# One transfer of a mask's diagonal blocks cut into four and spread between the large loads of a matmul-softmax kernel

## Chip, cores, metric

One core of a Trainium2 chip. The metric is device time of one execution in microseconds (us). A span of the profile is some 1.8 us shorter than the device time of the same execution.

## The reference

```python
batch, m, k, n = 16, 512, 512, 512
y = scale * np.matmul(x, weight)          # x [16, 512, 512], weight [512, 512], float32
y = np.where(mask == 1, y, -1e9)          # mask [512, 512], ones strictly below the diagonal
y_exp = np.exp(y - np.max(y, axis=-1, keepdims=True))
return y_exp / np.sum(y_exp, axis=-1, keepdims=True)
```

Input x is 16 MB, the output 16 MB, the weight 1 MB. Of the mask only the four diagonal blocks of 128 x 128 are read, 256 KB: the rest of it is known to both kernels.

## The kernel before

A unit is 1 MB of x: a half (256 rows) of two batches. There are 16 units, x0 to x15. For each, the SP queue loads 128 partitions x 8 KB, VectorE casts to bf16, TensorE transposes in 16 steps, VectorE and ScalarE evict half each, TensorE multiplies with the weight and adds the mask as one more product (`band`), ScalarE takes the exponential with its row sum, VectorE normalises, and the SP queue stores 1 MB.

The mask's path, with cuts:

```python
diag_r = bass.AP(tensor=mask.tensor, offset=mask.offset,
                 ap=[[N, P], [P * N + P, KT], [1, P]])   # 128 partitions, 4 rows of 512 B each
...
load(0)
seq(nc.sync.dma_start(diag_f32, diag_r))
seq(nc.sync.dma_start(w_f32, weight.rearrange("(p kt) n -> p kt n", kt=KT)))
for u in range(1, X_BUFS):                               # X_BUFS = 8
    load(u)
...
cast(0)
seq(nc.vector.tensor_scalar(out=diag_bf, in0=diag_f32, ...))     # 0/1 -> -512/0
transpose(0)
evict(0)
for t in range(T):
    # pm = spread[:, t] x diag_bf, then two copies of 64 rows into band
    ...
# casts of the weight, cast(1)
for u in range(U + 1):
    if u + 1 < U:
        transpose(u + 1)
    if u + 2 < U:
        cast(u + 2)
    if u + 1 < U:
        evict(u + 1)
    if u < U:
        multiply(u)
    if u >= 1:
        normalise(u - 1)
        store(u - 1)
        if u - 1 + X_BUFS < U:
            load(u - 1 + X_BUFS)
```

The softmax here doesn't subtract the row's maximum and nothing guards it: scores larger than these inputs give would overflow.

Of the kernel before, what the change touches and what calls it, by code (L numbers as in the profile page):

```python
# [8 lines left out]
FP32 = mybir.dt.float32  # L9
BF16 = mybir.dt.bfloat16  # L10
AF = mybir.ActivationFunctionType
ALU = mybir.AluOpType

MASK_NEG = -512.0
P = 128
X_BUFS = 8
# [5 lines left out]
def kernel(  # L22
# [15 lines left out]



    nc = tc.nc

    B, M, K = x.shape
    K2, N = weight.shape
    assert K == K2 and N == 512 and K == 512 and M == 512 and B % 2 == 0
    KT = K // P
    T = 4
    HP = P // 2
    HB = 2 * P
    U = B  # L50
# [7 lines left out]
    psum_y = ctx.enter_context(tc.tile_pool(name="psum_y", bufs=4, space=bass.MemoryType.PSUM))  # L58

    x_r = x.rearrange("(c e) (h p t) k -> c h p e (t k)", e=2, h=2, t=T)  # L60
    out_r = out.rearrange("(c e) (h p t) n -> c h p e (t n)", e=2, h=2, t=T)

    diag_r = bass.AP(tensor=mask.tensor, offset=mask.offset, ap=[[N, P], [P * N + P, KT], [1, P]])

    ident_bf = const.tile([P, P], BF16, name="ident_bf")
    w_f32 = const.tile([P, KT, N], FP32, name="w_f32")
    w_bf = const.tile([P, KT, N], BF16, name="w_bf")
    diag_f32 = const.tile([P, KT, P], FP32, name="diag_f32")
    diag_bf = const.tile([P, KT, P], BF16, name="diag_bf")
    spread = const.tile([P, T, P], BF16, name="spread")  # L70
    zeros = const.tile([P, N], BF16, name="zeros")
    band = const.tile([P, 2, T, HB], BF16, name="band")
# [3 lines left out]
    seq = tc.keep_in_program_order  # L76

    def load(u):
        xf = x_pool.tile([P, T, K], FP32, name="xf")
        seq(nc.sync.dma_start(xf.rearrange("p t k -> p (t k)"), x_r[u // 2, u % 2]))  # L80
        st_x[u] = xf

    def cast(u):
        xb = xb_pool.tile([P, T, K], BF16, name="xb")
        seq(nc.vector.tensor_copy(xb, st_x.pop(u)))  # L85
        st_xb[u] = xb

    def transpose(u):
        xb = st_xb.pop(u)
        st_pt[u] = [psum_t.tile([P, 2, T, P], BF16, name="pt") for _ in range(2)]  # L90
        for kt in range(KT):
            for t in range(T):
                seq(
                    nc.tensor.transpose(  # L94
                        st_pt[u][kt // 2][:, kt % 2, t],
                        xb[:, t].rearrange("p (k kt) -> p kt k", kt=KT)[:, kt],
                        ident_bf,
                    )
                )

    def evict(u):
        xt = xt_pool.tile([P, KT, T, P], BF16, name="xt")
        pt = st_pt.pop(u)
        seq(nc.vector.tensor_copy(xt[:, 0:2], pt[0]))  # L104
        seq(nc.scalar.copy(xt[:, 2:4], pt[1]))  # L105
        st_xt[u] = xt

    def multiply(u):
        h = u % 2
        NC = (h + 1) * HB  # L110
        xt = st_xt.pop(u)
        ot = ots[u % OUT_BUFS]
        rsum = sum_pool.tile([P, T], FP32, name="rsum")
        for t in range(T):
            py = psum_y.tile([P, N], FP32, name="py")
            for kt in range(KT):
                seq(
                    nc.tensor.matmul(  # L118
                        py[:, :NC],
                        lhsT=xt[:, kt, t],  # L120
                        rhs=w_bf[:, kt, :NC],
                        start=(kt == 0),
                        stop=(kt == KT - 1),
                    )
                )
            seq(
                nc.tensor.matmul(  # L127
                    py[:, h * HB : NC],
                    lhsT=ident_bf,
                    rhs=band[:, h, t],  # L130
                    start=False,
                    stop=True,
                    skip_group_check=True,
                )
            )
            seq(
                nc.scalar.activation(  # L137
                    out=ot[:, t, :NC],
                    in_=py[:, :NC],
                    func=AF.Exp,  # L140
                    bias=0.0,
                    scale=float(scale),
                    accum_out=rsum[:, t : t + 1],
                )
            )
        st_sum[u] = rsum

    def normalise(u):
        ot = ots[u % OUT_BUFS]
        NC = (u % 2 + 1) * HB  # L150
        rinv = sum_pool.tile([P, T], FP32, name="rinv")
        seq(nc.vector.reciprocal(rinv, st_sum.pop(u)))  # L152
        for t in range(T):
            seq(nc.vector.tensor_scalar_mul(ot[:, t, :NC], ot[:, t, :NC], rinv[:, t : t + 1]))  # L154
        if u % 2 == 0:
            seq(nc.gpsimd.memset(ot[0:2, 0, :HB], 1.0 / N))  # L156

    def store(u):
        ot = ots[u % OUT_BUFS]
        seq(nc.sync.dma_start(out_r[u // 2, u % 2], ot.rearrange("p t n -> p (t n)")))  # L160


    load(0)
    seq(nc.sync.dma_start(diag_f32, diag_r))  # L164
    seq(nc.sync.dma_start(w_f32, weight.rearrange("(p kt) n -> p kt n", kt=KT)))  # L165
    for u in range(1, X_BUFS):
        load(u)


# [13 lines left out]
    for g in range(2):  # L183
        for e in range(2):
# [4 lines left out]
                )  # L189
            )  # L190

    cast(0)
    seq(
        nc.vector.tensor_scalar(  # L194
            out=diag_bf,
            in0=diag_f32,
            scalar1=-MASK_NEG,
            scalar2=MASK_NEG,
            op0=ALU.mult,
            op1=ALU.add,  # L200
        )
    )
    transpose(0)
    evict(0)
    for t in range(T):
        pm = psum_y.tile([P, N], FP32, name="py")
        seq(
            nc.tensor.matmul(  # L208
                pm, lhsT=spread[:, t], rhs=diag_bf.rearrange("k b c -> k (b c)"), start=True, stop=True
            )  # L210
        )
        for g, copy in enumerate((nc.vector.tensor_copy, nc.scalar.copy)):
            half = slice(g * HP, (g + 1) * HP)
            src = pm.rearrange("p (h g c) -> p h g c", h=2, g=2)
            seq(copy(band[half, :, t, g * P : (g + 1) * P], src[half, :, g]))  # L215
    seq(nc.vector.tensor_copy(w_bf[:, 0:2], w_f32[:, 0:2]))
    seq(nc.scalar.copy(w_bf[:, 2:4], w_f32[:, 2:4]))
    cast(1)
# [1 line left out]
    for u in range(U + 1):  # L220
        if u + 1 < U:
            transpose(u + 1)
        if u + 2 < U:
            cast(u + 2)
        if u + 1 < U:
            evict(u + 1)
        if u < U:
            multiply(u)
        if u >= 1:
            normalise(u - 1)  # L230
            store(u - 1)
            if u - 1 + X_BUFS < U:
                load(u - 1 + X_BUFS)
# [35 lines left out]
```

## Time and profile before

| what | value | view |
|---|---|---|
| device time | 90.92 us (90.89 to 90.98) | three executions |
| span | 89.1 us | page |
| DMA moved | 34.95 MB, 392 GB/s over the span | page |
| DMA rate in the body | 416 to 438 GB/s | strip of 40 slices |
| TensorE busy | 72.0 us, 81% | page |
| last arithmetic, last landing | 82.0, 88.1 us | timeline, waits of the DMA queue |

How to read it: the strips cut the span into 40 slices of 2.2 us; a digit is a busy share in tenths. A stretch has its bounds and length first, then the busy time of each engine, and last the granted clock of TensorE, the DMA share and GB/s. In a timeline, a line is start, duration, engine, line of the kernel, operation, `out<-in`, and in brackets how long the engine had been idle and what ended that. The lines themselves stand in the prediction below.

Besides what those views show, the trace holds for every transfer 16 landing records, one for each DMA engine.

### The profile page before, as it was taken

The page shows a single profiled execution, that of the slowest core. Times are in us where ns is not written, and L with a number is a line of the kernel's source. Part 1 is how long each engine was busy: PE and PEld are TensorE (multiplying, and loading weights), DVE is VectorE, ACT ScalarE, POOL GpSimd, SP SyncE. Part 2 cuts the span into 40 slices and gives each one's busy share as a digit, 9 for nine tenths or more (in the row PEclk, how much of TensorE's full clock was granted, in tenths as well). Part 3 has the DMA queues.
Part 4 walks back from the last instruction along what each step waited for, and adds up shares of the span by engine and source line. Part 5 has one row for each costly group of instructions (what it writes and reads, how often), then busy time and mean ns, then how long its engine had stood idle before and what let it go on. Part 6 is the DMA issues. An engine that isn't in the chain of part 4 may idle for free.

```text
span 89.1 us, 1610 instructions
## 1 busy us (share of the span) xinstructions
PE 72.0 (81%) x584; PEld 49.4 (56%) x592; DVE 60.5 (68%) x123; ACT 55.3 (62%) x154; POOL 7.3 (8%) x20
## 2 busy tenths in 40 slices
PE   4996205999999999999999999999999999960000
PEld 1325005767489569758955975795598578520000
DVE  5885914756849959994996899599685948607000
ACT  5403830646779778687977877797687869660000
POOL 7620000000100200020020002001000100200000
PEclk9999995559999999999999999999999999998555
DMA  0859999999999999999999999999999999999970
GB/s 11 324 204 381 419 434 427 423 423 430 416 419 419 423 430 430 419 419 423 423 427 430 430 416 419 430 434 423 416 427 430 419 416 430 438 416 434 423 313 22
DMA packets 5287, 34.95 MB, mean 392 GB/s; under 512 B 545, under 2 KB 1057, under 8 KB 1057
## 3 DMA queue, kind: packets, MB, share of 16 engines
q1 hardware_dynamic: 5280, 34.87, 93.9%
q8 instruction: 4, 0.07, 0.3%
q14 instruction: 3, 0.02, 0.0%
HBM read 18.09 MB, written 16.78 MB: 391 GB/s over the span
## 4 chain that ended last, share of the span: by engine, by line
PE 73%; DMA 12%; DVE 3%; SPq 2%; issue 1%; ACT 1%; DVEq 0%; ACTq 0%
PE py L118 48%; PE pt L94 16%; DMA xf<-in_x_dram 12%; PE py L127 8%; DVE ot L154 1%; DVE xb L85 1%; SPq L80 1%; ACT ot L137 1%; SPq L164 1%; SPq L165 1%; DVEq L264 0%; DVE rinv L152 0%; ACTq L264 0%
## 5 line engine op out<-in xcount | busy, mean ns | idle before, releaser
L118 PE MATMUL py<-w_bf,xt 128*128 128x256 bf16 (+1 forms) x248 | 51.0, 333 | 0.4
L137 ACT ACTIVATE ot<-py 128x256 f32<-128x256 f32 (+1 forms) x64 | 31.2, 493 | 8.9 <-PE py L127 8.8
L118 PEld LDWEIGHTS <-xt 128*128 128x128 bf16 x256 | 25.2, 101 | 12.7
L105 ACT COPY xt<-pt 128x1024 bf16<-128x1024 bf16 x16 | 16.2, 1013 | 14.7 <-PE pt L94 10.1
L154 DVE TENSOR_SCALAR ot<-ot,rinv 128x256 f32<-128x256 f32 (+1 forms) x64 | 23.5, 431 | 0.8
L85 DVE CAST xb<-xf 128x2048 bf16<-128x2048 f32 x16 | 19.5, 1220 | 5.9 <-DMA xf<-in_x_dram 5.9
L94 PE MATMUL pt<-ident_bf,xb 128*128 128x128 bf16 x256 | 17.8, 225 | 5.3 <-DVE xb L85 5.3
L94 PEld LDWEIGHTS <-xb 128*128 128x128 bf16 x256 | 16.6, 115 | 7.7 <-DVE xb L85 6.7
L127 PE MATMUL py<-band,ident_bf 128*128 128x256 bf16 x64 | 18.0, 281 | 0.0
L104 DVE COPY xt<-pt 128x1024 bf16<-128x1024 bf16 x16 | 11.0, 688 | 8.9 <-PE pt L94 8.9
L137 ACT ACTIVATION_READ_ACCUMULATOR ot<-py 128x1 f32 x64 | 12.8, 200 | 0.0
L156 POOL MEMSET ot<- 2x256 f32 x8 | 3.6, 448 | 67.7 <-DVE ot L154 67.7
L127 PEld LDWEIGHTS <-ident_bf 128*128 128x128 bf16 x64 | 6.5, 101 | 4.4
L173 PE MATMUL py<-zeros 128*128 128x512 bf16 x12 | 5.3, 632 | 1.2 <-DVE zeros L170 1.2
L152 DVE RECIPROCAL rinv<-rsum 128x4 f32<-128x4 f32 x16 | 2.7, 169 | 3.2 <-ACT ot L137 3.2
L179 DVE MEMSET ot<- 128x1024 f32 x4 | 3.6, 912 | 0.6 <-issue 0.6
L173 PEld LDWEIGHTS <-zeros 128*128 128x128 bf16 x12 | 1.6, 144 | 3.9 <-issue 2.8
L186 ACT ACT_TABLE_LOAD x1 | 1.3, 1283 | 0.7 <-PEq L250 0.7
L215 ACT CAST band<-py 64x256 bf16<-64x256 f32 x4 | 1.4, 368 | 0.2 <-DVE band L215 0.2
L215 DVE CAST band<-py 64x256 bf16<-64x256 f32 x4 | 1.4, 406 | 0.0
L208 PE MATMUL py<-diag_bf,spread 128*128 128x512 bf16 x4 | 1.0, 377 | 0.4 <-DVE diag_bf L194 0.4
L180 POOL MEMSET ot<- 2x256 f32 x4 | 1.2, 302 | 1.5 <-DVE ot L179 1.4
(14 smaller groups left out, 6.6 us busy)
## 6 DMA issues: line engine op xcount, KB each, us to landing
xf<-in_x_dram SPq DMA_DIRECT2D x16, 1024.0 KB, 13.9
out_dram<-ot SPq DMA_DIRECT2D x16, 1024.0 KB, 10.6
w_f<-in_weight_dram SPq DMA_DIRECT2D x1, 1024.0 KB, 8.4
diag_f<-in_mask_dram SPq DMA_DIRECT2D x1, 256.0 KB, 6.5
```

Of the source, the lines that this page charges most:

```text
L85: seq(nc.vector.tensor_copy(xb, st_x.pop(u)))
L94: nc.tensor.transpose(st_pt[u][kt // 2][:, kt % 2, t], xb[:, t].rearrange("p (k kt) -> p kt k", kt=KT)[:, kt], ident_bf,)
L104: seq(nc.vector.tensor_copy(xt[:, 0:2], pt[0]))
L105: seq(nc.scalar.copy(xt[:, 2:4], pt[1]))
L118: nc.tensor.matmul(py[:, :NC], lhsT=xt[:, kt, t], rhs=w_bf[:, kt, :NC], start=(kt == 0), stop=(kt == KT - 1),)
L127: nc.tensor.matmul(py[:, h * HB : NC], lhsT=ident_bf, rhs=band[:, h, t], start=False, stop=True, skip_group_check=True,)
L137: nc.scalar.activation(out=ot[:, t, :NC], in_=py[:, :NC], func=AF.Exp, bias=0.0, scale=float(scale), accum_out=rsum[:, t : t + 1],)
L154: seq(nc.vector.tensor_scalar_mul(ot[:, t, :NC], ot[:, t, :NC], rinv[:, t : t + 1]))
L156: seq(nc.gpsimd.memset(ot[0:2, 0, :HB], 1.0 / N))
L173: seq(nc.tensor.matmul(idle, lhsT=zeros[:, :P], rhs=zeros, start=True, stop=True))
L179: nc.vector.memset(ots[i][:, :, HB:], 0.0)
L215: seq(copy(band[half, :, t, g * P : (g + 1) * P], src[half, :, g]))
```

## The change

Its intent: the mask's small packets should not stand in one block ahead of the weight, and the first products should need only half of it.

```diff
-    load(0)
-    seq(nc.sync.dma_start(diag_f32, diag_r))
-    seq(nc.sync.dma_start(w_f32, weight...))
-    for u in range(1, X_BUFS):
-        load(u)
+    def load_mask(b):
+        r = slice(b * P, (b + 1) * P)
+        seq(nc.sync.dma_start(diag_f32[:, b], mask[r, r]))
+
+    load(0)
+    load_mask(0)
+    seq(nc.sync.dma_start(w_f32, weight...))
+    load_mask(1)
+    load(1)
+    load_mask(2)
+    load(2)
+    load_mask(3)
+    for u in range(3, X_BUFS):
+        load(u)
 ...
+    def spread_mask(h):
+        blocks = slice(2 * h, 2 * h + 2)
+        # scale of these two blocks; 4 products of 256 columns; 4 copies into band[:, h]
+        ...
     cast(0)
-    # scale of all four blocks
     transpose(0)
     evict(0)
-    # 4 products of 512 columns, 8 copies into band
+    spread_mask(0)
     # casts of the weight, cast(1)
 ...
         if u + 1 < U:
             transpose(u + 1)
+        if u == 0:
+            evict(1)
         if u + 2 < U:
             cast(u + 2)
-        if u + 1 < U:
+        if 0 < u < U - 1:
             evict(u + 1)
         if u < U:
             multiply(u)
+        if u == 0:
+            spread_mask(1)
```

Below, the four pieces are m0 to m3, the weight is w.

More of the change, by code (lines that the diff above doesn't have):

```diff
@@ L61 @@
     out_r = out.rearrange("(c e) (h p t) n -> c h p e (t n)", e=2, h=2, t=T)
-    diag_r = bass.AP(tensor=mask.tensor, offset=mask.offset, ap=[[N, P], [P * N + P, KT], [1, P]])
     ident_bf = const.tile([P, P], BF16, name="ident_bf")
@@ L190 @@
             )
-    cast(0)
-    seq(
-        nc.vector.tensor_scalar(
-            out=diag_bf,
-            in0=diag_f32,
-            scalar1=-MASK_NEG,
-            scalar2=MASK_NEG,
-            op0=ALU.mult,
-            op1=ALU.add,
-        )
-    )
+    def spread_mask(h):
+        blocks = slice(2 * h, 2 * h + 2)
+        seq(
+            nc.vector.tensor_scalar(
+                out=diag_bf[:, blocks],
+                in0=diag_f32[:, blocks],
+                scalar1=-MASK_NEG,
+                scalar2=MASK_NEG,
+                op0=ALU.mult,
+                op1=ALU.add,
+            )
+        )
+        for t in range(0, T, 2):
+            pm = psum_y.tile([P, N], FP32, name="py")
+            for j in range(2):
+                seq(
+                    nc.tensor.matmul(
+                        pm[:, j * HB : (j + 1) * HB],
+                        lhsT=spread[:, t + j],
+                        rhs=diag_bf[:, blocks].rearrange("k b c -> k (b c)"),
+                        start=True,
+                        stop=True,
+                    )
+                )
+            src = pm.rearrange("p (t g c) -> p t g c", t=2, g=2)
+            for g, copy in enumerate((nc.vector.tensor_copy, nc.scalar.copy)):
+                half = slice(g * HP, (g + 1) * HP)
+                seq(copy(band[half, h, t : t + 2, g * P : (g + 1) * P], src[half, :, g]))
+    cast(0)
     transpose(0)
     evict(0)
-    for t in range(T):
-        pm = psum_y.tile([P, N], FP32, name="py")
-        seq(
-            nc.tensor.matmul(
-                pm, lhsT=spread[:, t], rhs=diag_bf.rearrange("k b c -> k (b c)"), start=True, stop=True
-            )
-        )
-        for g, copy in enumerate((nc.vector.tensor_copy, nc.scalar.copy)):
-            half = slice(g * HP, (g + 1) * HP)
-            src = pm.rearrange("p (h g c) -> p h g c", h=2, g=2)
-            seq(copy(band[half, :, t, g * P : (g + 1) * P], src[half, :, g]))
+    spread_mask(0)
     seq(nc.vector.tensor_copy(w_bf[:, 0:2], w_f32[:, 0:2]))
```

## The prediction

> **What bounds the kernel now.** I read three things in this order: the chain of work that ended last, the waits of the DMA queue at the end, and the busy time and bytes stretch by stretch. The first points at the wrong engine, so it has to be checked against the other two.
>
> The page of the kernel before, the chain and the strips of its second part:
>
> ```profile
> PE 73%; DMA 12%; DVE 3%; SPq 2%; issue 1%; ACT 1%; DVEq 0%; ACTq 0%
> ...
> PEclk9999995559999999999999999999999999998555
> DMA  0859999999999999999999999999999999999970
> GB/s 11 324 204 381 419 434 427 423 423 430 416 419 419 423 430 430 419 419 423 423 427 430 430 416 419 430 434 423 416 427 430 419 416 430 438 416 434 423 313 22
> ```
>
> The chain gives TensorE 73%, but the DMA strip is at 9 from the fourth slice (6.7 us) to the last but two, at 416 to 438 GB/s. Both look full. The tail decides. These are the stretches of one us at the end, then the waits of the DMA queue:
>
> ```profile
> 81.00:82.00 1.00, 0.00 (x0) 0.00 (x0) 0.96 (x3) 0.00 (x0) 0.00 (x0) 0.83 0.97 410
> 82.00:83.00 1.00, 0.00 (x0) 0.00 (x0) 0.00 (x0) 0.00 (x0) 0.00 (x0) 0.50 1.01 426
> 83.00:84.00 1.00, 0.00 (x0) 0.00 (x0) 0.00 (x0) 0.00 (x0) 0.00 (x0) 0.50 1.03 434
> 84.00:85.00 1.00, 0.00 (x0) 0.00 (x0) 0.00 (x0) 0.00 (x0) 0.00 (x0) 0.50 1.03 434
> 85.00:86.00 1.00, 0.00 (x0) 0.00 (x0) 0.00 (x0) 0.00 (x0) 0.00 (x0) 0.50 0.87 369
> 86.00:87.00 1.00, 0.00 (x0) 0.00 (x0) 0.00 (x0) 0.00 (x0) 0.00 (x0) 0.50 0.41 172
> ```
> ```profile
> SPq L264 <- DMA out_dram<-ot: 5.5, 1, 5.5
> ...
> SPq L80 <- DMA diag_f<-in_mask_dram: 1.3, 1, 1.3
> ```
>
> The last two columns are DMA share and GB/s. All arithmetic is over at 82.0 us, when the last store is issued. From 82 to 87 the DMA still moves 426+434+434+369+172 = 1.84 MB, of which the last store is only 1.05 MB. So about 0.8 MB was queued in front of it: the end is set by a transfer queue that has been full since about 7 us, and TensorE runs beside it with a little slack. That slack: the last store takes 6.0 us from issue (82.04) to landing (88.08 = 82.04 + 0.5 of issue + 5.5 of wait), and the quickest 1 MB transfer of the trace, x0 into an empty queue, takes 5.0. Compute could end about 1 us later for free.
>
> Where is the queue not full? At the start. VectorE waits for each load in turn, so its timeline shows the landings:
>
> ```profile
> 5.79 1.23 DVE L85 CAST xb<-xf 128x2048 bf16<-128x2048 f32 x1 [0.36 <-DMA xf<-in_x_dram]
> 8.04 0.43 DVE L194 TENSOR_SCALAR diag_bf<-diag_f 128x512 bf16<-128x512 f32 x1 [1.02 <-DMA diag_f<-in_mask_dram]
> ...
> 10.54 0.69 DVE L216 CAST w_bf<-w_f 128x1024 bf16<-128x1024 f32 x1 [0.15 <-DMA w_f<-in_weight_dram]
> 13.02 1.23 DVE L85 CAST xb<-xf 128x2048 bf16<-128x2048 f32 x1 [1.79 <-DMA xf<-in_x_dram]
> 15.50 1.23 DVE L85 CAST xb<-xf 128x2048 bf16<-128x2048 f32 x1 [1.26 <-DMA xf<-in_x_dram]
> ```
>
> x0 lands at 5.79, the mask at 8.04, the weight at 10.54, x1 at 13.02, x2 at 15.50. A 1 MB transfer costs 2.48 to 2.50 us, and the mask, a quarter of that, 2.25. At the full rate it would be 262 KB / 425 GB/s = 0.62. The stretches of half a us say why:
>
> ```profile
> 5.50:6.00 0.50, 0.50 (x3) 0.09 (x1) 0.21 (x1) 0.00 (x0) 0.29 (x1) 1.00 0.56 148
> 6.00:6.50 0.50, 0.50 (x2) 0.00 (x0) 0.50 (x1) 0.00 (x0) 0.00 (x0) 1.00 0.43 103
> 6.50:7.00 0.50, 0.00 (x0) 0.00 (x0) 0.50 (x1) 0.00 (x0) 0.00 (x0) 1.00 0.35 88
> 7.00:7.50 0.50, 0.42 (x8) 0.43 (x9) 0.02 (x1) 0.00 (x0) 0.00 (x0) 1.00 1.11 389
> ```
>
> While the mask moves, the engines are busy only 0.35 to 0.56 of the time. They wait between packets; the packets themselves are not that slow. From 6.0 to 7.0 they moved (103+88) x 0.5 = 95 KB, 187 packets of 512 B, in (0.43+0.35) x 0.5 x 16 = 6.2 us of engine time: 33 ns a packet. The mask has 512 packets, 32 on each of 16 engines: 32 x 33 = 1.06 us busy, so some 1.2 of its 2.25 us are gaps.
>
> **What the Trainium skill says.** "DMA: Bandwidth & Descriptors", Specifications, gives a fabric ceiling of 435 GB/s; the strip's 416 to 438 sits on it, so only the start has anything to give. The same page, Queues, rings and completion order: each engine consumes its descriptors in ring order; the landings above, one after another in order of issue, agree. Thus what a small transfer costs is paid by everything behind it. Its Rules for kernel authors advise coalescing small transfers, since under 64 KB overhead dominates; four pieces of 64 KB go the other way, and the trace can't yet say whether that holds in a full queue. "TensorE: Matmul & The Clock Gate", Part 1, has the clock halved after an idle window of about 3.4 us; here TensorE idles from 9.54 to 14.30 us, and the clock is 0.50 from 13.4 to 20.
>
> **The change part by part.**
>
> Transfers. One of 256 KB becomes four of 64 KB, same bytes, still 512 B rows, 128 of them each, 8 per engine. Order: x0, m0, w, m1, x1, m2, x2, m3, x3 and on. If the gaps are time in which small packets aren't ready soon enough, the large neighbours (2.48 us each) cover them, and a piece costs its busy time: 8 x 33 ns = 0.27 us. Four are 1.06 us in place of 2.25: the queue gains 1.2 us. I take 0.2 off for gaps that remain at the seams: 1.0 us. This lies on the path that sets the end, all of it.
>
> x1 has only two pieces ahead of it: 13.02 - 2.25 + 2 x 0.27 = 11.3 us, 1.7 earlier. Its weight lands at 10.54 - 2.25 + 0.27 = 8.6.
>
> Issues. Three more, about 0.6 us of the SP queue each (0.57 for the mask now); they delay nothing, for the transfers are 2.5 us apart. In the kernel before, the tenth issue waited 1.3 us for the second transfer to land, so about eight can be outstanding. With thirteen, x3 waits for x0 (5.8 us), x5 for w (8.6), x7 for x1 (11.3); the queue then holds x1 and more. It should not run dry.
>
> Compute. The mask work goes from 1 scale, 4 products of 512 columns and 8 copies of 64x256 to 2 scales, 8 products of 256 and 8 copies of the same size: equal within some 0.3 us. Half of it moves behind the first products. The first half waits for m1, about 8.9 us, then scale 0.25, products 0.5, two copies per engine 0.8: done near 10.5; the weight's casts (0.69 and 1.04) by 11.6. The cast of x1 runs 11.4 to 12.6 and its transposes start near 12.7 in place of 14.30. TensorE's idle time shrinks from 4.8 to under 3 us, so the clock may stay full, which saves about half of the 5.7 us that it is busy at 0.5 between 13 and 20. The first eviction also no longer waits behind the third cast (16.64 in the trace; it would be at about 13.3). The first store then leaves near 20 in place of 23.05. This is 3 us of compute, but it lies beside the full queue: it makes the slack larger, and does not move the end. Later, two casts already wait for their loads (0.8 and 1.0 us, at 63.5 and 68.4), so the lead is spent waiting for x14 and x15.
>
> Sum: 90.92 - 1.0 = 89.9 us, 1.1% faster.
>
> **The rivals.**
> 1. *The gaps belong to 512 B rows wherever they stand.* Then a piece costs 2.25/4 = 0.56 us, nothing is saved, and the time stays at 90.9; with a start-up stall in each piece, up to 91.4. For it: the busy share is low even though the mask was issued at 1.5 us and had 3 us in which to get ready. Against: the share falls and rises in the course of it (0.56, 0.43, 0.35), which looks like waiting for a supply that large neighbours would hide. About 25%.
> 2. *The pieces vanish wholly,* at 0.15 us each: 1.65 us saved, 89.3. For it: 33 ns may overstate a packet, as 512 B at the full rate of an engine would be 19 ns. About 15%.
> 3. *TensorE is the bound,* as the chain says. Then the 3 us of earlier compute show, and the time is about 88. Against: 0.8 MB stand before the last store, and the DMA strip has no hole for 80 us. Under 5%.
> 4. *The eight outstanding transfers starve the queue,* now that four places are taken by small ones: a hole of a us or two in the first 15 us, time 91 to 92. Against: the count above. About 4%.
>
> **Range and chances.** The bound makes it narrow: 2.25 - 0.62 = 1.6 us is all that the mask can give back, and that is 1.8%, under the 2% (1.82 us). To be faster by over 2% something else must help too: 4%. To be slower by over 2%, a new hole must open: 2%. Within 2%: 94%. Prediction 89.9 us, 89.3 to 90.7 for 8 in 10.
>
> **What would show it.** Right: in the timeline of VectorE the cast of x1 begins near 11.3 us and that of x3 near 17.1 (now 18.07); the strip shows no slice near 204 GB/s after x0; SP's wait for the last store grows to 7 us or more, as compute ends at 79 us or earlier with the queue unmoved but for 1 us. Clock: fewer slices at 5. Rival 1: the cast of x1 near 11.9 and that of x3 still at 18. Rival 3: the last wait stays 5.5 us and the end moves with TensorE. Rival 4: the DMA share drops below 0.5 in some stretch between 6 and 20 us. What would make it wrong outright: a rate other than 425 GB/s in the body, or an engine that is held up on its own, for the slowest engine sets each landing.

## More of the kernel before

A reading used throughout the experiments is *the x4 mark*: the mean of the 16 landings of x4, the sixth 1 MB transfer. It says how far the queue has got once all of the mask is through. In the kernel before it is 20.10 us.

## The result, and the profile after

The changed kernel ran at 90.55 us (90.46 to 90.62, four runs), the kernel before on the same occasion at 90.95 (90.89 to 91.12). The ratio is 0.9952 with a 95% interval of 0.9935 to 0.9970. Ratios here are the mean time of one kernel's fast runs over the mean of the other's fast runs of the same rounds, so not quite the ratio of the medians quoted. The change is worth 0.4 us: the direction and the bound were as predicted, the size (1.05 us from 90.95) was two and a half times too large.

The page of the changed kernel, strips:

```profile
PEclk9999655899999999999999999999999999997555
DMA  0899999999999999999999999999999999999970
GB/s 15 306 373 384 381 376 428 417 432 428 414 425 417 425 436 428 402 417 432 428 428 417 428 421 421 425 436 425 421 417 432 425 421 425 428 432 428 425 306 26
```

The slice of 204 GB/s is gone, as predicted. In its place four slices in a row (4.4 to 13.3 us) stand at 373 to 384, where the kernel before had 204, 381, 419 and 434. The one deep hole has become several shallow ones. TensorE's clock is still halved for a while.

The timeline of VectorE at the start of the changed kernel:

```profile
6.18 1.23 DVE L83 CAST xb<-xf 128x2048 bf16<-128x2048 f32 x1 [0.75 <-DMA xf<-in_x_dram]
8.14 0.69 DVE L102 COPY xt<-pt 128x1024 bf16<-128x1024 bf16 x1 [0.73 <-PE pt L92]
9.37 0.29 DVE L202 TENSOR_SCALAR diag_bf<-diag_f 128x256 bf16<-128x256 f32 x1 [0.53 <-DMA diag_f<-in_mask_dram]
...
12.03 1.23 DVE L83 CAST xb<-xf 128x2048 bf16<-128x2048 f32 x1 [0.25 <-DMA xf<-in_x_dram]
14.39 0.69 DVE L102 COPY xt<-pt 128x1024 bf16<-128x1024 bf16 x1 [1.14 <-PE pt L92]
```

x1 is cast at 12.03, against 13.02 before: one us earlier, not the 1.7 predicted; that is near the sign of the prediction's rival 1 (11.9). The first scale, which waits for m1, begins at 9.37 (8.9 predicted). The sign that was set on x3 could not be read: its cast starts at 18.92, later than the 18.07 of before, because VectorE does the mask's second half ahead of it, while x3 itself has landed on the last engine at 17.57 (17.98 before).

The half-us stretches of the changed kernel in which the pieces m0, m1, m2 and m3 pass:

```profile
5.50:6.00 0.50, 0.50 (x3) 0.09 (x1) 0.00 (x0) 0.00 (x0) 0.29 (x1) 1.00 1.19 425
8.00:8.50 0.50, 0.50 (x10) 0.43 (x8) 0.36 (x1) 0.00 (x0) 0.00 (x0) 1.00 0.69 238
11.00:11.50 0.50, 0.00 (x0) 0.00 (x0) 0.50 (x2) 0.44 (x2) 0.00 (x0) 0.50 0.64 235
14.00:14.50 0.50, 0.50 (x8) 0.50 (x6) 0.11 (x1) 0.00 (x0) 0.00 (x0) 0.50 1.03 379
```

Here is the surprise. Around m1 and m2 the DMA share falls to 0.69 and 0.64, with a 1 MB transfer queued behind each of them. The gaps that the large neighbours were to cover are partly still there. But not at all four pieces: around m0 and m3 the share is 1.19 and 1.03.

The waits of the DMA queue in the changed kernel:

```profile
SPq L284 <- DMA out_dram<-ot: 7.1, 2, 4.7
SPq L78 <- DMA xf<-in_x_dram: 2.3, 2, 1.7
...
SPq L78 <- DMA w_f<-in_weight_dram: 1.7, 1, 1.7
```

At the end the queue waits 7.1 us for the output, against 5.5 before: arithmetic ends at 80.0 us in place of 82.0, two us earlier, while the last landing moves only from 88.08 to 87.73. That is the mark of a kernel bound by its transfers. The other two lines are issues held up until an early load has landed (about eight transfers may be outstanding, by the prediction's count); the strip has no hole there.

The body runs at the same rate in both. The stretch from 22 to 40 us, before and then after:

```profile
22.00:40.00 18.00, 17.89 (x156) 12.63 (x157) 15.17 (x33) 14.25 (x42) 1.35 (x3) 1.00 1.01 422
```

```profile
22.00:40.00 18.00, 18.00 (x171) 13.21 (x170) 15.18 (x31) 13.98 (x41) 0.90 (x2) 1.00 1.01 421
```

So the whole difference is made at the start. The x4 mark moved from 20.10 to 19.74 us, the mean landing of the last store from 86.87 to 86.55, the time by 0.40.

### The profile page after: what moved, and what is told of

It is laid out like the page before. It is cut to its first block, busy times and chain, and to the rows that moved or that the text cites. A ratio compares the mean times of both kernels' runs of the same rounds, so it can differ in the third digit from the quotient of the medians.

```text
span 88.8 us, 1632 instructions
## 1 busy us (share of the span) xinstructions
PE 71.3 (80%) x596; PEld 49.3 (56%) x596; DVE 60.6 (68%) x124; ACT 55.2 (62%) x154; POOL 7.3 (8%) x20
## 4 chain that ended last, share of the span: by engine, by line
PE 72%; DMA 10%; DVE 3%; SPq 2%; ACT 1%; DVEq 0%; issue 0%; ACTq 0%
PE py L116 47%; PE pt L92 16%; DMA xf<-in_x_dram 10%; PE py L125 8%; DVE ot L152 1%; DVE xb L83 1%; SPq L163 1%; SPq L78 1%; ACT ot L135 1%; PE py L215 0%; SPq L167 0%; DVEq L284 0%; DVE rinv L150 0%; ACTq L284 0%
## 5 line engine op out<-in xcount | busy, mean ns | idle before, releaser
L116 PE MATMUL py<-w_bf,xt 128*128 128x256 bf16 (+1 forms) x256 | 50.0, 329 | 0.0
L154 POOL MEMSET ot<- 2x256 f32 x8 | 3.6, 448 | 65.7 <-DVE ot L152 65.7
L215 PE MATMUL py<-diag_bf,spread 128*128 128x256 bf16 x8 | 1.6, 339 | 1.2 <-DVE diag_bf L202 1.2
L215 PEld LDWEIGHTS <-spread 128*128 128x128 bf16 x8 | 0.9, 111 | 1.5 <-issue 1.3
## 6 DMA issues: line engine op xcount, KB each, us to landing
out_dram<-ot SPq DMA_DIRECT2D x16, 1024.0 KB, 11.9
```

The lines of the kernel that those rows point to most:

```text
L116: nc.tensor.matmul(py[:, :NC], lhsT=xt[:, kt, t], rhs=w_bf[:, kt, :NC], start=(kt == 0), stop=(kt == KT - 1),)
L154: seq(nc.gpsimd.memset(ot[0:2, 0, :HB], 1.0 / N))
```

## The experiments

The theory after the result, *stride*: gaps belong to the mask's rows, 512 B long and 2 KB apart in memory, wherever they stand; the change hid only a part of them. The rivals: *supply* (many small packets in a row are not made ready fast enough; this is what the prediction rested on), *neighbours* (the seams between small and large transfers cost), *compute* (the new order of the arithmetic made or ate the gain), and *chance* at the start. 17 runs were made, on several chips, each set with the kernel before on the same chip.

The measured values of all, to be referred to below. "x4" is the x4 mark; "end" is the landing of the last store, mean of the 16 engines and last engine; times are medians of the fast executions, with their range where it is wide. The kernel before ran at 90.87 to 90.97 in the sets of the variants; ratios are to the runs of the same set.

```
kernel                   x4      end: mean  last    time us                 ratio to before (95%)
before                   20.10   86.87   88.08      90.95                   1
before_again             20.22   86.97   88.20      91.0 (one)              -
after (the change)       19.74   86.55   87.73      90.55                   0.9952 (0.9935-0.9970)
after_again              19.84   86.62   87.93      90.60                   0.9960 (0.9946-0.9975)
after_warm               19.73   86.58   87.75      90.51                   0.9959 (0.9947-0.9971)
late_first_store         19.72   86.57   88.21      92.07 (91.04-92.32)     1.0110 (1.0071-1.0149)
split_transfers_only     (profile of 413 us)        94.90 (94.70-95.56)     1.0453 (1.0422-1.0485)
split_transfers_only_b   19.67   91.79   93.06      95.86 (one)             -
order_only               20.07   87.11   89.31      91.03 (90.78-92.08)     1.0026 (0.9986-1.0066)
four_in_a_row            20.13   87.12   88.87      91.36 (90.97-92.33)     1.0065 (1.0016-1.0115)
two_pieces               20.07   86.86   88.10      90.89                   0.9989 (0.9977-1.0001)
one_on_act_queue         19.81   88.29   90.42      93.21                   1.0247 (1.0227-1.0266)
rows_1k                  19.90   86.78   88.57      91.08                   1.0011 (0.9996-1.0026)
strided_512              19.88   86.66   87.86      90.61                   0.9966 (0.9954-0.9977)
mixed_512                20.83   87.61   88.84      91.08                   1.0006 (0.9993-1.0019)
dense_512                19.12   86.07   88.21      90.99 (90.69-91.52)     1.0007 (0.9981-1.0034)
dense_one                19.08   86.16   88.25      90.95 (90.74-91.58)     1.0007 (0.9983-1.0032)
no_mask_transfer         18.24   85.50   86.68      90.12 (89.33-90.49)     0.9894 (0.9858-0.9931)
no_mask_warm             18.14   86.00   88.23      90.48 (90.07-90.89)     0.9953 (0.9930-0.9977)
```

All gave a correct result.

### Again, unchanged: before_again and after_again

No edit.

> The kernel before, unchanged, for a second profile. After the change x0 landed 0.39 us later (cast of x0 at 6.18 against 5.79), and the forecast had no term for it. Theory 'chance': where x0 lands varies from execution to execution by some 0.4 us, so this profile shows its first cast anywhere from 5.6 to 6.2. Rival 'caused': the small transfers behind x0 hold it up, and this profile shows the first cast at 5.8 within 0.1, the mask 2.25 after it, the weight 2.5 after that.

> The changed kernel, unchanged. 'Chance': the first cast moves by more than 0.2 us from 6.18. 'Caused': it stays at 6.18 within 0.1. In both: pieces and large transfers as in the first profile, x3 landing about 11.4 us after x0 (12.2 before), and 0.3 to 0.5 us faster than the kernel before.

The last engine's landing of x0 was 5.77 and 5.91 us in two profiles of the kernel before, 6.16 and 6.07 in two of the changed one, and 5.75 and 5.80 in order_only and split_transfers_only, which begin with the same transfers as before and after respectively. The transfers behind x0 do not decide it, so "caused" is refuted as a fixed delay; "chance" was only half right, since the change repeats within 0.1. It matters little: the x4 mark is 20.1 to 20.2 with the head of before and 19.7 to 19.9 with that of after, however x0 landed. The gain repeated: 0.9960.

### Transfers alone: split_transfers_only, and once more as _b

```diff
-    seq(nc.sync.dma_start(diag_f32, diag_r))        # kernel before
-    ...
+    load_mask(0) ... load_mask(3)                   # where the change has them; arithmetic as before
```

> The four small transfers in their new places, with the arithmetic in the order of before (whole mask spread ahead of the weight's casts). Theory 'queue': the end is set by the transfer queue alone, so this gives the whole gain: 90.55, ratio 0.995 to 0.996, though compute starts later than in the changed kernel. Rival 'compute': the earlier arithmetic made some of the gain; then this is slower than the changed kernel by 0.2 us or more.

> The transfers of the change with the arithmetic of before, once more, because its first profile fell in an execution of 413 us with a TensorE at a fraction of its clock, and its times of 94.7 to 95.6 contradicted 'queue'. New theory 'arithmetic waits for the last piece': the whole mask is scaled before the first eviction in the order of VectorE, so the first eviction waits for m3 (15.2 us) in place of 8.0; compute then ends near 86.5 in place of 82.0 and the last store, with nothing queued before it, lands 5 us later. The profile should show the first eviction after 15.5 us and a last wait below 5 us. Rival: the transfers themselves are slower; then the DMA strip has holes.

One of its six executions took 414.9 us, and the first profile fell into that one: 12 products of 512 columns took 15.8 us there. That execution is left out. The others took 94.7 to 95.6 us, so the expectation was wrong by more than 4 us. The second profile says why. VectorE's timeline of split_transfers_only_b:

```profile
5.91 1.23 DVE L85 CAST xb<-xf 128x2048 bf16<-128x2048 f32 x1 [0.47 <-DMA xf<-in_x_dram]
15.15 0.43 DVE L203 TENSOR_SCALAR diag_bf<-diag_f 128x512 bf16<-128x512 f32 x1 [8.01 <-DMA diag_f<-in_mask_dram]
15.49 0.68 DVE L104 COPY xt<-pt 128x1024 bf16<-128x1024 bf16 x1
```

Its page, the strip of the DMA:

```profile
DMA  0899999999924999999999999999999999999970
```

The scale of the whole mask stands ahead of the first eviction in VectorE's order and waits 8 us for m3. Everything after it is late, stores included, and the DMA strip gets a hole (2 and 4 tenths) from 26 to 31 us, where the loads are used up and no store is ready: the first one is issued at 28.36 us. This is the new theory "arithmetic waits for the last piece", and its rival is out as well, since the x4 mark is 19.67, as in the changed kernel. Two things follow. The new order of the arithmetic is no gain of its own but the condition for cutting the mask. And the arithmetic has no slack of seven us; whether it has the one us that the prediction gave it was not tested.

### Order alone: order_only

```diff
-    load_mask(0) ... load_mask(3)                   # changed kernel
+    seq(nc.sync.dma_start(diag_f32, diag_r))        # one transfer after x0, as before
```

> One transfer of the whole mask where it was, with the arithmetic in the new order (second half of the mask behind the first products, second eviction ahead of the third cast). 'Queue': nothing is gained, 90.95, ratio 0.999 to 1.001, and the last wait for the output grows. 'Compute': 90.7 or less. For the start: by 'caused' the first cast is at 5.8 as before, by 'chance' anywhere.

Ratio 1.0026, interval 0.9986 to 1.0066: the new order alone gains nothing, as "queue" has it. Two of six runs took 92.1 and 92.2 us (the latter over 1.5% above the fastest, so not counted as fast), which neither theory expects; more of that below.

### How much the mask costs: no_mask_transfer

```diff
-    load_mask(0) ... load_mask(3)
+    nc.gpsimd.memset(diag_f32, 1.0)
+    # affine_select per block: 1 strictly below the diagonal; right for this mask only
```

> The changed kernel without any mask transfer; the diagonal blocks are made on chip (right for this mask only). It measures all that the mask costs the queue. In the kernel before the mask landed 2.25 us after x0 in the profile; if that is its whole price, this runs at 90.9 - 2.2 = 88.7 and the four pieces still cost some 1.8 of it (90.55 - 88.7). If the forecast's price of four pieces (1.06 + 0.2 us) was right and something else held the changed kernel up, this runs at 89.3.

The x4 mark is 18.24 us (18.14 in no_mask_warm). Against a mean of 18.19, the whole mask costs the queue 20.13 - 18.19 = 1.94 us (mean of before, before_again and order_only), and the four pieces in their places 19.76 - 18.19 = 1.57 (mean of the six profiles in the table with those pieces). The difference, 0.37 us, is the gain. The stretch from 5 to 18 us shows the same to the eye. Before, after, and without mask:

```profile
5.00:18.00 13.00, 7.31 (x50) 4.67 (x49) 7.75 (x12) 4.91 (x9) 0.30 (x1) 0.82 0.94 382
```

```profile
5.00:18.00 13.00, 8.12 (x62) 5.82 (x61) 7.33 (x11) 5.23 (x11) 0.30 (x1) 0.74 0.99 396
```

```profile
5.00:18.00 13.00, 8.79 (x69) 6.40 (x68) 7.57 (x12) 5.70 (x13) 0.83 (x4) 0.74 1.02 427
```

14 GB/s over 13 us are 0.18 MB, and at 425 GB/s 0.43 us; the step to no mask is 31 GB/s, more than twice as large. The pieces left most of the price standing.

The time fell short of the mark: 0.85 us gained in place of 1.9, with a wide spread. See the last part of this section.

### Is it the cut or the neighbours? four_in_a_row and two_pieces

```diff
-    load_mask(0); w; load_mask(1); load(1); load_mask(2); load(2); load_mask(3)
+    load_mask(0) ... load_mask(3); w; load(1) ...                  # four_in_a_row
+    load_two(0); w; load(1); load_two(1); load(2) ...              # two_pieces, two blocks each
```

> The four pieces one after the other where the whole mask was, ahead of the weight; arithmetic as in the changed kernel. Theory 'neighbours': the large transfers between the pieces hide the gaps, so without them the mask costs 2.2 us again: 90.9. Rival 'slicing': the cut itself helps; then 90.5 as the changed kernel.

> The changed kernel with two pieces of 128 KB (two blocks each) in place of four of 64 KB: one between x0 and the weight, one between x1 and x2. In one transfer the mask cost 1.9 us of the queue, in four pieces 1.55. If it is the neighbours that hide part of each piece's gaps, two pieces lie between: x4 at 19.9 to 20.0, 90.6 to 90.75. If the gaps come mostly at the start of each piece, two pieces are cheaper than four: x4 below 19.75, 90.5 or less.

Four pieces in a row: the mark is 20.13, as with one transfer. The cut itself gives nothing; what helps is the large neighbour. (The time, 91.36, is even longer; three of six runs were 91.7 to 92.3.) Two pieces: 20.07, and 90.89 us, no gain: the mark is inside the scatter of the kernels with one transfer (20.07 to 20.22). So one further place between large transfers hides nothing that can be seen, three hide 0.37 us. "Neighbours" is right in kind, and far smaller than the prediction took it; that more or smaller pieces hide more was not tested further.

### What the rows cost: strided_512, dense_512, dense_one, mixed_512

In these the mask is made on chip as above, and the transfers are read by nobody; only where their rows lie in memory differs.

```diff
+    # strided_512, places of the change: the very rows of the change, 2 KB apart
+    seq(nc.sync.dma_start(unread[:, b], mask[b*P:(b+1)*P, b*P:(b+1)*P]))
+    # dense_512, same places: 128 rows of 512 B from one stretch of 64 KB
+    seq(nc.sync.dma_start(unread[:, b], mask[b*32:(b+1)*32, :].rearrange("r (q c) -> (r q) c", c=P)))
+    # dense_one: one transfer after x0, 512 rows of 512 B from one stretch of 256 KB
+    #   ap=[[P, P], [P * P, KT], [1, P]]
+    # mixed_512, places of the change: 32 partitions x the rows of all four blocks
+    #   ap=[[N, 32], [P * N + P, KT], [1, P]]
```

> Mask made on chip; four pieces of 64 KB in the places of the change, with rows of 512 B as there but from one dense stretch of memory, read by nobody. Theory 'row size': what a piece costs comes from its 128 packets of 512 B; this runs as the changed kernel, 90.5. Rival 'stride': it comes from rows that lie 2 KB apart; then a piece costs about 0.2 us and this runs at 0.8 us over the kernel without mask transfer.

> Control for the dense pieces: mask made on chip, the very transfers of the change (four pieces, rows 512 B long and 2 KB apart), read by nobody. The landing of x4, as the mean over the 16 engines in the landing records, was 20.1 to 20.2 us in the kernel before, 19.8 with the change, 19.1 with dense pieces, 18.2 without mask. Theory 'stride': 19.8 here, as in the changed kernel. Rival 'who makes the mask': 19.1, as with dense pieces; then the dense run showed nothing about stride. The time is no sure guide, since single runs of such variants came out 1.2 us late after the start: 90.4 to 91.6.

> Mask made on chip; one transfer of 256 KB where the whole mask was, 512 rows of 512 B from one dense stretch, four to a partition, read by nobody. 'Stride': the gaps of the whole mask come from rows 2 KB apart, so here there are none, the piece costs about 0.9 us and x4 lands at 19.1 to 19.2 in the mean. Rival 'supply': 512 small packets in a row aren't made ready fast enough, so the gaps stay, the piece costs 2.0 and x4 lands at 20.1.

> Mask made on chip; four pieces in the places of the change, each a quarter of the partitions with the rows of all four diagonal blocks (32 x 4 rows of 512 B, four different offsets within 2 KB), read by nobody. If what costs is that all 128 rows of a piece start at the same offset within 2 KB, this is near the dense pieces: x4 at 19.1 to 19.4. If rows 2 KB apart cost whatever their offset, x4 at 19.8.

strided_512 is the control: 19.88 us and 90.61, as the changed kernel, so it doesn't matter who makes the mask. dense_512 comes to 19.12, a price of 0.93 us or 0.23 a piece; dense_one, 512 small packets in one block just as in the kernel before, to 19.08, a price of 0.89. With dense rows there is no difference between one transfer and four, and the block's packets, which run until 6.56 us, leave no gaps. The stretches of half a us in which the block of dense_one passes, and the next one, with one dip of the share behind it:

```profile
5.50:6.00 0.50, 0.12 (x1) 0.00 (x0) 0.00 (x0) 0.00 (x0) 0.32 (x2) 1.00 1.25 349
6.00:6.50 0.50, 0.00 (x0) 0.00 (x0) 0.38 (x1) 0.00 (x0) 0.00 (x0) 1.00 1.21 450
6.50:7.00 0.50, 0.00 (x0) 0.00 (x0) 0.50 (x1) 0.00 (x0) 0.00 (x0) 1.00 0.76 313
```

Compare the prediction's lines of the kernel before, with 0.56, 0.43 and 0.35 in the same stretches. So "supply" is refuted, and the packets' number and size are not the trouble: where the rows lie in memory is. Rows 2 KB apart cost 1.94 - 0.89 = 1.05 us more than dense ones in one block and 1.57 - 0.93 = 0.64 in four pieces. (They also cover four times the stretch of memory; the runs don't separate the two.) By the *time*, the expectation of dense_512 went to "row size" (90.99, not below the changed kernel); its mark says the opposite, and dense_one confirms the mark. I trust the mark here because it is taken right where the mask ends, and because the loss that follows occurs without any mask too.

mixed_512 gave no support to its theory: 20.83, a price of 2.64, far from the dense pieces and dearer than one transfer. But its profile fell in the slowest of its six executions (91.59; the others took 90.88 to 91.16), so the price of the others is probably lower. Why the mixed pieces are this dear is open.

The landing records show one thing more, and it limits what "stride" explains. Take a piece and the large transfer behind it, from mean landing to mean landing, less the 2.485 us of a large transfer alone. As the mean of the six profiles with the mask's own rows, m0 to m3 cost 0.35, 0.46, 0.65 and 0.17 us; in dense_512 they cost 0.27, 0.22, 0.23 and 0.17. (The sums, 1.63 and 0.89, are not quite the 1.57 and 0.93 of the marks, since x0 landed at slightly different times.) Nearly all of the extra price lies at m1 and m2. m3, whose rows lie 2 KB apart too, costs no more than a dense piece in any of the six. Nor do the packets themselves take longer: the median is 27 ns with dense rows and with the mask's own. So in these runs only transfers with rows 2 KB apart have the gaps, but not all of them do, and what the engines wait for at m1 and m2 is open.

### Other ways to load it: one_on_act_queue and rows_1k

```diff
-    load_mask(0) ... load_mask(3)
+    seq(nc.scalar.dma_start(diag_f32, diag_r))      # one_on_act_queue: whole mask, Activation queue, first
 
-        seq(nc.sync.dma_start(diag_f32[:, b], mask[r, r]))
+        c = b // 2 * HB                             # rows_1k: rows of 1 KB, half of it unused
+        seq(nc.sync.dma_start(diag_f32[:, b], mask[b * P : (b + 1) * P, c : c + HB]))
```

> The whole mask as one transfer, issued from the Activation queue at the start, so that its packets mix with those of x0 and the weight on another ring; arithmetic as in the changed kernel. 'Neighbours': the gaps are filled by the large packets beside them, the mask costs only its busy time of about 0.9 us, and this runs at 89.6 to 89.8, with x0 landing up to 1 us later. Rival 'the small packets slow what stands beside them': 90.4 to 90.6, no better than the four pieces.

> The changed kernel, each piece reading rows of 1 KB (both blocks' columns of its half) in place of 512 B: 512 KB of mask, twice the bytes, half of which nobody uses; one more scale. A right result for the mask assumed by both kernels. At the full rate the pieces cost 4 x 0.31 = 1.24 us of the queue, against the 1.55 measured for the strided 512 B. If longer rows escape what the stride costs, x4 lands at 19.5 in the mean and the time is 90.2 to 90.3. If rows 2 KB apart cost the same again on top of their bytes, x4 at 20.0 or later and 90.7 or more.

On a queue of its own the mask costs 1.62 us of the x4 mark, no less than in pieces, and the first load waits for it. VectorE's first cast in one_on_act_queue:

```profile
8.93 1.23 DVE L84 CAST xb<-xf 128x2048 bf16<-128x2048 f32 x1 [3.50 <-DMA xf<-in_x_dram]
```

Three us late, the first store leaves at 24.64, and the time is 93.21. Both expectations missed; this is worse than either. Rows of 1 KB move twice the bytes for a mark of 19.90, a price of 1.71: half a us above the 1.24 at full rate. Longer rows lose less to the stride but not enough to pay for their bytes. The time, 91.08, is half a us above the changed kernel's, more than the mark accounts for; in its profile the last engine ends 1.8 us behind the mean one (1.2 in the changed kernel).

### What happens after the start: late_first_store, no_mask_warm, after_warm

Six variants so far, besides rows_1k and the late split_transfers_only, ran slower than their x4 mark promises (order_only, four_in_a_row, one_on_act_queue, dense_512, dense_one, no_mask_transfer). In them the rate from 22 to 40 us was 381 to 419 GB/s in place of 421 to 423, and in these profiles the first store had left more than 3.4 us after the x4 mark, in the others at most 3.0. Was the late store the cause?

```diff
+        if u == 1:                                  # late_first_store: changed kernel, 1.8 us on VectorE
+            for _ in range(2):
+                seq(nc.vector.memset(delay, 0.0))
 
-WARM = 12
+WARM = 14                                           # after_warm, no_mask_warm
+    keep_warm(4)                                    # products on zeros behind the first transposes
+    keep_warm(8)                                    # and behind the first half of the mask
```

> The changed kernel with two idle memsets on VectorE (0.91 us each) ahead of the first normalisation, so the first store leaves about 1.8 us later, near 24.0, 4.2 us after x4 has landed. In twelve profiles the rate from 22 to 40 us was 421 to 423 GB/s where the first store left at most 3.0 us after the mean landing of x4, and 381 to 419 where it left 3.4 us or more after. Theory 'late store': here the rate falls to 419 or less and the time rises by 0.2 to 1.2 us to 90.8 to 91.8, though the start is untouched. Rival 'only company': late stores and low rate have another cause in common; then the rate stays at 421 and the time at 90.55, as the queue still holds x6 and x7.

> No mask transfer, and 14 more products on zeros in TensorE's idle stretches before the first products, so that its clock is not halved there; the first store then leaves earlier, near 20 us, under 3 us after x4. 'Late store': the rate from 22 to 40 us comes back to 421 and the time falls from 90.12 with its wide spread (89.33 to 90.49) to 89.0 to 89.3 with a narrow one, so that the whole 1.6 to 1.9 us of the mask show. 'Only company': 90.1 as before.

> The changed kernel with the same 14 products. Its first store is early enough already, so by 'queue' the time stays at 90.5 within 0.15 although compute runs up to 2 us earlier; the last wait for the output grows. If TensorE's halved clock cost the changed kernel anything, it falls to 90.2 or less.

late_first_store went the way of "late store" in time (92.07, 1.5 us slower than the changed kernel), with the start untouched (mark 19.72). Its profiled execution was the fastest of the six (91.04) and shows little: 420 GB/s, the mean end as in the changed kernel, the last engine 0.3 to 0.5 us later. no_mask_warm spoke against it: its first store left at 19.74, 1.6 us after the mark, and the rate still broke down, to 254 GB/s for two us:

```profile
22.00:24.00 2.00, 2.00 (x23) 1.83 (x22) 1.97 (x6) 2.00 (x8) 0.00 (x0) 1.00 1.06 385
24.00:26.00 2.00, 1.95 (x21) 1.28 (x20) 1.97 (x5) 1.53 (x4) 0.01 (x1) 1.00 0.97 254
26.00:28.00 2.00, 2.00 (x12) 1.03 (x11) 1.98 (x4) 1.43 (x5) 0.44 (x1) 1.00 0.96 401
```

The DMA share is near 1.0 there, so the engines had work and their packets took longer (those of the large transfers 0.50 us in the mean from 24 to 26 us, in place of 0.31). So a late store can lose time here, but an early one does not prevent the loss, and what slows the packets between the last loads and the first stores stays open. Neither the kernel before nor the changed one shows it in any of their four profiles, so it does not enter their difference.

after_warm behaved as "queue" says. Its page:

```profile
PEclk9999999999999999999999999999999999995555
```

With the clock never halved the first store leaves at 21.00 in place of 22.20, and the time is 90.51, as before the products were added. Arithmetic that is earlier still buys nothing.

## Why the prediction was right or wrong

**What bounds it: right.** The chain's 73% TensorE did not mean a TensorE bound. Arithmetic ended 2.0 us earlier and the end moved by 0.35; a clock that is not halved at the start (after_warm) and the new order alone (order_only) moved nothing.

**The term that was mis-sized: the gain of the queue, 2.25 - 1.06 - 0.2 = 1.0 us; measured 1.94 - 1.57 = 0.37.** It fell at both ends.
- *The whole mask, 2.25.* That was read from one landing to the next on VectorE, that is, between the last of 16 engines each time. The mean engine's step is 5.63 to 7.67, 2.04 us, and taking the transfer away gives 1.94. 0.3 us of the error.
- *The pieces, 1.06 + 0.2.* "The large neighbours (2.48 us each) cover them, and a piece costs its busy time: 8 x 33 ns = 0.27 us." This step failed: large transfers on both sides do not cover the gaps of this mask. Dense pieces do cost about that (0.23), but the mask's own cost 0.39 in the mean, because the gaps come with rows 2 KB apart and not with small packets as such. 0.3 us of the error. What the engines wait for, and why nearly only at m1 and m2, stays open. The prediction's rival 1 (25%) was right that gaps travel with the rows, wrong that 512 B rows have them wherever they stand (dense ones have none), and overstated it: not all of the 1.2 us of gaps stayed, but some 0.64.
- The argument that turned me from rival 1 (the share falls and rises, which looks like waiting for a supply) was no evidence: the view does not tell what the engines wait for.

**The transfer's place, and x1: right in kind.** x1 came 1.0 us earlier, not 1.7, by the same two errors and because x0 itself landed 0.16 us later in the mean in that profile.

**Compute: too hopeful, without effect.** The clock was halved after all (fifth to eighth slice). The prediction went by the length of the gap, under 3 us in place of 4.8; the gap did shrink, to 2.6, but the clock fell at 9.48 us, before that gap began, and since the first product no idle stretch had been longer than 1.2. In the 3.41 us up to there TensorE was busy for 1.36. (In the kernel before, 3.41 us with 2.11 busy kept the full clock, and the next 3.41, wholly idle, halved it at 13.4.) The first eviction of x1 came at 14.39 in place of 13.3, and the first store at 22.20, not 20. None of it lies on the path.

**Rival 2** (pieces vanish) and **rival 3** (TensorE bound) are refuted by the same numbers. **Rival 4** (few outstanding transfers starve the queue): the waits of 2.3 and 1.7 us on loads exist, the strip has no hole. **The cap** of 1.6 us on what the mask can give back held, and with it the judgement "within 2%".

## What to carry to other kernels

When a transfer is slow and its engines are half idle, find out what they wait for before promising that neighbours will fill the gaps: send the same packets from dense memory, and send nothing, and compare how far the queue has got right behind them. Measure the price of a transfer by removing it, not from the distance of two landings, which mixes in the spread of 16 engines. And cutting a transfer pays only if no instruction in front of the critical work waits for the last piece: here the cut without the new order cost 4.5%.

## What the Trainium skill lacked or had wrong

- "DMA: Bandwidth & Descriptors", Rules for kernel authors, advises coalescing small transfers, under 64 KB above all. Here four pieces of 64 KB between large loads cost 1.57 us of the queue and one of 256 KB 1.94; with dense rows both cost 0.9, and four pieces in a row cost as much as one transfer. In this queue the cut into 64 KB, just at the page's limit, had no price that the runs show.
- The same page, Latency and other measured facts, has row pitches from 512 KiB up, for tiles of 16 KiB a partition. No page has a price for short rows at a small pitch: 512 B every 2 KB cost 0.39 us per 64 KB between large loads (0.17 to 0.65 by the piece), dense rows 0.23; a whole block of 256 KB 1.94 against 0.89. What the engines wait for is not shown.
- No page says what a fetch of instructions costs the transfers of a full queue. In the kernel before, a 16 KB instruction transfer at 23.9 us held one DMA engine for 1.1 us; the lag of the last engine behind the first grew from 0.7 to 2.1 us at the next landing, and at the end the last engine is 1.2 us behind the mean one. In the changed kernel the same transfer stands at 21.5 us, and the lag grows at the landing after it, too. That the two belong together is inferred from the moment.
- "TensorE: Matmul & The Clock Gate", Part 1, warns that the clock has been seen stuck at a quarter for 50 us and more. One execution here (split_transfers_only, 414.9 us) looks like that: 1.32 us for each of its first 12 products of 512 columns, three times the 0.44 of the same products in the kernel before, and a span of 413 us. But its trace holds no record of the clock, so that it was the clock is inferred.
- No page says how little work it takes to have the clock halved. The prediction's reading, a gap as long as the idle window, does not fit: in the changed kernel TensorE was busy for 1.36 of the 3.41 us before the clock fell, and not idle for more than 1.2 us at a stretch.
- No page explains the packets that took 0.50 us in the mean in place of 0.31 between the last loads and the first stores (254 GB/s for two us in no_mask_warm, 381 over 18 us in one_on_act_queue).
